# A hybrid decoder layer: the down projection's weight sums on GpSimd's queue, larger operand loads, and a reordered last block

## The chip, the cores and the metric

One core of a Trainium2 chip. The metric is the device time of one execution in microseconds (us); lower is better. Engines: PE (TensorE, matmuls), DVE (VectorE), ACT (ScalarE), POOL (GpSimd) and SP (SyncE), which here only issues DMAs. DMAs are issued in the order of the issuing engine's queue; "SPq" and "POOLq" are those of SP and POOL.

## The reference

One layer on x of 2048 x 1024, float32. Attention and a convolution group share one input projection; their outputs, concatenated, go through one output projection; then comes a SwiGLU network (inner size 2816), which is most of the work.

```python
y = rms_norm(x, g1); u = y @ w_in            # q, k, v and the conv group's input
a = sliding_window_attention(q, k, v, ...)   # window 128, 8 heads on 2
c = conformer_conv(u_conv, ...)              # GLU, depthwise width 31, LN, swish, pointwise
h = x + rms_norm(concat(a, c) @ w_out, g2)
z = rms_norm(h, g3)
f = (silu(z @ w_gate) * (z @ w_up)) @ w_down
out = h + rms_norm(f, g4)
```

## The kernel before, in words

Every float32 product is made of three matmuls of a short format: high times high, high times low, low times high. ACT makes the high part of an operand (line 888), DVE or POOL subtracts it to get the low part (line 892); both together are called a split. The network's products use Strassen's scheme in Winograd's form: seven block products for eight, with sums of blocks as operands. So sums of weight blocks and of activations are needed, and DVE does most of them.

The rows go through the network in two halves. Stages, with the letters that follow @ in names: A projections, B attention, C convolution, J and W the output side, H the split rows for the network, F0 gate/up of the first half (about 650 to 973 us), G0 its down projection (about 964 to 1285), then F2 and G2 for the second half. F keeps its products in DRAM (`mids`, accumulators in `keeps`) and G loads them. Small tasks run in lanes beside a stage, each with a rate at which its instructions are mixed in. One of them, `stage_tsums`, runs in F0: for each of 11 pairs of weight row blocks it loads four blocks of `w_down` (line 1187: two halves of a "wx" tile and two "fc" tiles, 256 KB each), subtracts four times on DVE (line 85) and stores each sum to the DRAM tensor `td` (line 1193), which G0 and G2 read as weights. "wx" has one buffer, "fc" three, so the next pair's loads wait for this pair's stores to land.

A scheduler fixes the order of instructions on each engine ahead of time, by priorities and its own picture of when operands are there. Each engine then runs its list in order, SP too: an SP instruction that waits holds everything behind it. `tied` only gives an instruction a place behind a stage's leading matmul in that order; `after_first(a, b)` orders b behind a.

In `stage_p2` (G), `load(i)` fetches the operand of step i from `mids` (line 1237), before into "at" for the first two steps and "fa" after ("fa" has 4 buffers, which F's stores use too), in G2 into "fc"; weights come in pairs into "mb" or "raw". `split(i)` makes the operand tiles for PE. For the last six steps of G2 the loop order is turned around, so that one block of 128 rows after another is complete; its epilogue takes the sum of squares on ACT (line 1358), multiplies by the gain `gbs[1]`, takes a reciprocal square root of a single column in ten small DVE operations (`rsqrt_one`), and scales and adds the residual twice. `finish` is the epilogue of the other blocks.

Of the kernel before, what the change touches and what calls it, by code (L numbers as in the profile page):

```python
# [13 lines left out]
F32R = mybir.dt.float32r  # L14
BF16 = mybir.dt.bfloat16
I8 = mybir.dt.int8
I32 = mybir.dt.int32
AF = mybir.ActivationFunctionType
ALU = mybir.AluOpType
# [4 lines left out]
D = 1024  # L24
DFF = 2816
P = 128
T = 512
# [5 lines left out]
EPS = 1e-6  # L33
# [4 lines left out]
def layer_kernel(ctx, tc, x, xT, cols, rows, sinks, relb, onehot, w_in, w_four, w_pw, w_out, w_gate, w_up, w_down, out):  # L38
    nc = tc.nc
    ctx.enter_context(nc.allow_non_contiguous_dma(reason="broadcast and skewed constant loads"))  # L40
    cst = ctx.enter_context(tc.tile_pool(name="cst", bufs=1))
# [7 lines left out]
    def nm(s):  # L49
        uid[0] += 1  # L50
        return f"{s}@{lab[0]}_{uid[0]}"
# [3 lines left out]
    def t_(tag, shape, dt=F32):  # L55
        return sb.tile(list(shape), dt, tag=tag, name=nm(tag), bufs=BUFS[tag])
# [4 lines left out]
    def f2(tag, shape=(P, T)):  # L61
        return t_(tag, shape)

    def hl(tag):
        return t_(tag, (P, 2, T), F32R)
# [13 lines left out]
    act = nc.scalar.activation  # L79
# [3 lines left out]
    def dve(op):  # L83
        def emit(*args, **kw):
            r = op(*args, **kw)  # L85
            if not paced[0]:
                pace["main"] = r.ins
            elif pace["main"] is not None and pace["main"] is not pace["tied"]:
                tc.add_manual_dep(
                    r.ins,  # L90
                    pace["main"].name,
                    mybir.DependencyInfo(mybir.DependencyClass.NoSync, mybir.DependencyReason.DATA),
                    reason="conv taps keep pace with the projections",
                )
                pace["tied"] = pace["main"]
            return r

        return emit

    stt = dve(nc.vector.scalar_tensor_tensor)  # L100
    vtt = dve(nc.vector.tensor_tensor)
    vts = dve(nc.vector.tensor_scalar)
    ptt = nc.gpsimd.tensor_tensor
# [9 lines left out]
    def tied(r):  # L113
        if lead_pe[0] is not None and lead_pe[0] is not r:
            after_first(lead_pe[0], r)
        return r
# [49 lines left out]
                stt(y, t, 1.5, y, ALU.add, ALU.mult)  # L166
        return y

    def rsqrt_one(a, b):
        v, y, w, vs = (sm(1) for _ in range(4))  # L170
        stt(v, a, EPS, b, ALU.add, ALU.add)
        vts(y.bitcast(I32), v.bitcast(I32), 1, None, ALU.logical_shift_right)
        vts(y.bitcast(I32), y.bitcast(I32), -1, 0x5F3759DF, ALU.mult, ALU.add)
        vts(vs, v, -(2.0**-13), None, ALU.mult)
        for f, d in ((v, -3.0), (v, -12.0), (vs, 3 * 2.0**-5)):
            stt(w, y, f, y, ALU.mult, ALU.mult)
            stt(y, w, d, y, ALU.add, ALU.mult)
        return y

    def after_first(first, r, how=mybir.DependencyClass.NoSync):  # L180
        tc.add_manual_dep(
            r.ins,
            first.ins.name,
            mybir.DependencyInfo(how, mybir.DependencyReason.DATA),
            reason="order",
        )
# [12 lines left out]
    ident = cst.tile([P, P], F32, name="ident")  # L199
    make_identity(nc, ident)  # L200
    NCOL = cols.shape[1]
    colt = cst.tile([P, NCOL], F32, name="colt")
    nc.sync.dma_start(colt, cols)
    x0, w0 = [], []
    for i in range(4):
        xt = f4("x", (P, 2, T))
# [34 lines left out]
    )  # L241
    kz = cst.tile([P, 2, P + T], F32R, name="kz")
    nc.gpsimd.memset(kz[:, :, 0:P].bitcast(F32), 0.0)
    junk = cst.tile([P, D], BF16, name="junk")
    vtok = cst.tile([P, 5, P], F32, name="vtok")


# [639 lines left out]
    def split_f(x, w):  # L887
        act(w[:, 0], x, AF.Copy)  # L888
        return w
# [290 lines left out]
    def stage_tsums(td):  # L1180
        L = "G0"
        for pr in range(NF // 2):
            lab[0] = L
            wx = f4("wx", (P, 2, T))
            b = [wx[:, 0], wx[:, 1], f2("fc"), f2("fc")]
            for i, (f, n) in enumerate(((0, 0), (0, 1), (1, 0), (1, 1))):
                tied(nc.sync.dma_start(b[i], w_down[2 * pr + f, :, n * T : (n + 1) * T]))
            yield 5
            b11, b12, b21, b22 = b
            for to, o, p_, q_ in ((0, b11, b12, b11), (2, b12, b22, b12), (1, b22, b22, b11), (3, b21, b21, b22)):  # L1190
                lab[0] = L
                vtt(o, p_, q_, ALU.subtract)
                nc.sync.dma_start(td[to, pr], o)
                yield 1

    def finish(L, gb, jobs, pool=True):
        lab[0] = L
        n_ = len(jobs)
        ssq = sm(4)
        for j, (rows_, halves) in enumerate(jobs):  # L1200
            for n in range(2):
                act(junk[:, 0:T], halves[n], AF.Square, scale=D**-0.5, accum_out=ssq[:, 2 * n + j : 2 * n + j + 1])
                vtt(halves[n], halves[n], gb[n], ALU.mult)
            yield 2.0
            lab[0] = L
        vtt(ssq[:, 0:n_], ssq[:, 0:n_], ssq[:, 2 : 2 + n_], ALU.add)
        r = rsqrt(ssq[:, 0:n_], n_, 1, pool and L == "G0")
        for j, (rows_, halves) in enumerate(jobs):
            ht = f4("wx" if L == "G0" else "mid")
            nc.sync.dma_start(ht, h_scr[rows_])  # L1210
            for n in range(2):
                cs = slice(n * T, (n + 1) * T)
                stt(halves[n], halves[n], r[:, j : j + 1], ht[:, cs], ALU.mult, ALU.add)
                nc.sync.dma_start(out[rows_, cs], halves[n])
            yield 2.0
            lab[0] = L

    def stage_p2(ws, am, td, last=False):
        L = f"G{ws[0]}"
        lab[0] = L  # L1220
        npr = NF // 2
        banks = [mm() for _ in range(4)]
        steps = [(ty, pr) for ty in range(7) for pr in range(npr)]
        rawa, rawb, opsd = {}, {}, {}

        def source(ty, pr):
            if ty in (0, 1, 6):
# [4 lines left out]
        def load(i):  # L1232
            if i < len(steps):
                lab[0] = L
                ty, pr = steps[i]
                rawa[i] = f2("fc" if last else "at" if i < 2 else "fa")
                nc.sync.dma_start(rawa[i], am[ty, pr])
                if pr % 2 == 0:
                    rb = t_("raw" if last else "mb", (P, 2, T))
                    for j in range(min(2, npr - pr)):  # L1240
                        nc.sync.dma_start(rb[:, j], source(ty, pr + j))
                        rawb[i + j] = rb[:, j]

        def split(i):
            if i < len(steps):
                lab[0] = L
                b = split_f(rawb[i], hl(("ql" if i >= len(steps) - 4 else "w") if last else "hl"))
                lo(rawb.pop(i), b, False)
                a = split_f(rawa[i], hl("hl"))
                lo(rawa.pop(i), a, False)  # L1250
                opsd[i] = a, b

# [19 lines left out]
        sse = sm(4) if last else None  # L1272
        gbs = []
# [48 lines left out]
                    lf.add(f"E{ws[0]}.{b}", finish(L, gbs, [  # L1322
                        (rows_of(j, 0), (home("c11", "x", j), home("c12", "p", j))) for j in (b - 1, b)], False))

        LAST = 6 if last else 0
        nn = len(steps) - LAST
        for i in range(3):
            load(i)
        split(0)
        split(1)  # L1330
        for i in range(nn):
            ty, pr = steps[i]
            load(i + 3)
            if i + 2 < nn + (LAST > 0):
                split(i + 2)
            for b in range(4):
                lab[0] = L
                chain(i, b, ty == 0 and pr == 0, pr == npr - 1)
                if pr == npr - 1:
                    after(ty, b)  # L1340
                yield 0.69
            del opsd[i]
        if not last:
            return
        for i in range(nn + 3, len(steps)):
            load(i)
        for i in range(nn + 1, len(steps)):
            split(i)
        hts = []
        for b in range(4):  # L1350
            hts.append(f4("chl"))
            nc.sync.dma_start(hts[b], h_scr[rows_of(b, 0)])
        for b in range(4):
            lab[0] = L
            for i in range(nn, len(steps)):
                chain(i, b, False, i == len(steps) - 1)
            ssq = sm(1)
            act(junk[:, 0:T], banks[b], AF.Square, scale=D**-0.5, accum_out=ssq)
            g = f2("fa")
            vtt(g, banks[b], gbs[1], ALU.mult)  # L1360
            yield 0.69 * LAST
            lab[0] = L
            r = rsqrt_one(ssq, sse[:, b : b + 1])
            c = home("c11", "x", b)
            for y, n in ((c, 0), (g, 1)):
                cs = slice(n * T, (n + 1) * T)
                stt(y, y, r, hts[b][:, cs], ALU.mult, ALU.add)
                nc.sync.dma_start(out[rows_of(b, 0), cs], y)

    clk = [0.0]  # L1370
# [69 lines left out]
    PRE_S0, PRE_S2 = 22, 16  # L1440
    H1, H2, H3, H4 = 0, 4, 7, 11
    NH = 24
    JL, JS = 10, 2
    lb = Lane(RB, 0)
    lc = Lane(RC0, LC)
# [75 lines left out]
    td = dr.tile([4, NF // 2, P, T], F32, name="td")  # L1521
    keeps = [dr.tile([PRES[2 * i], P, T], F32, name=f"keeps{i}") for i in range(2)]
    ws, ops = (0, 1), {}
    for n, off in (("B11", 0), ("B21", 4)):
        lh.add(n + ".0", stage_h_plain(ws, ops, n, off), lambda: since(lw, "W0", NH))
    run(stage_w(1, True, 2, "mid", "hl", "at", mm, norm=lambda g: lh.add("N1", g)))
# [85 lines left out]
```

## Time and profile before

| | |
|---|---|
| median of 3 runs | 1929.01 us (1927.28 to 1930.13) |
| profiled execution | 1926.44 us, span 1924.7 us |
| PE busy | 1891.3 us (98%), mean clock granted 0.997 |
| DVE busy | 1492.3 us (78%) |
| ACT busy | 970.1 us (50%) |
| POOL busy | 197.0 us (10%) |
| DMA | 439.35 MB, 228 GB/s on average |

A group or timeline row gives start and length in us, the engine, the line, out<-in by tile names with @stage, and in brackets the engine's idle time before it and what ended that. L85 is the helper that records all of DVE's operations, and L108 all matmuls, so tiles tell them apart. In the rows of a stretch, the busy time of each engine stands with its instruction count in parentheses.

### The profile page before, as it was taken

The numbers are of one execution on the slowest core, as the hardware profiler recorded it, in microseconds if no ns is written. First come the engines' busy times: TensorE is split into PE (matmuls) and PEld (weight loads), VectorE is DVE, ScalarE is ACT, GpSimd is POOL, SyncE is SP. The second block draws the span as 40 slices with busy tenths as digits, with TensorE's granted clock in tenths as the row PEclk, the third lists the DMA queues.
The fourth block names the chain that finished last, engine by engine and source line by source line (L and its number), as shares of the span: only waits on it lengthen the run. The fifth ranks groups of instructions, "written<-read, shape, count | busy, mean of one in ns | idle before, by whom it ended". The sixth has DMA issues, their size and how long they took to land.

```text
span 1924.7 us, 26694 instructions
## 1 busy us (share of the span) xinstructions
PE 1891.3 (98%) x8714; PEld 1531.9 (80%) x8714; DVE 1492.3 (78%) x2796; ACT 970.1 (50%) x1911; POOL 197.0 (10%) x263
## 2 busy tenths in 40 slices
PE   9999999999999999999999999999999999999998
PEld 7777777777778888887877878888888888888886
DVE  6999999887876999988988765787566665455557
ACT  5366445557567433333445573676434333345443
POOL 2010012110000000000000010010033233211000
PEclk9999999999999999999999999999999999999999
DMA  9886757669668775787496696699544543376664
GB/s 332 303 290 229 228 175 225 195 222 340 216 237 282 247 260 188 252 301 239 146 310 217 214 328 219 230 343 324 174 170 151 167 142 121 120 246 193 206 194 156
DMA packets 227707, 439.35 MB, mean 228 GB/s; under 512 B 22728, under 2 KB 48752, under 8 KB 227568
## 3 DMA queue, kind: packets, MB, share of 16 engines
q1 hardware_dynamic: 206256, 403.04, 63.3%
q10 hardware_dynamic: 19392, 28.32, 4.0%
q0 software_dynamic: 1920, 6.29, 0.8%
q8 instruction: 68, 1.11, 0.2%
q14 instruction: 71, 0.58, 0.1%
HBM read 318.54 MB, written 119.02 MB: 227 GB/s over the span
## 4 chain that ended last, share of the span: by engine, by line
PE 75%; DMA 11%; DVE 9%; issue 2%; ACT 1%; SPq 1%; POOL 0%; DVEq 0%; ACTq 0%; POOLq 0%
PE mm@F L108 36%; PE mm@G L108 20%; PE mm@A L108 9%; PE tr@W L108 4%; DVE fc@C L85 2%; PE tr@B L108 2%; PE mm@W L108 2%; PE ct@J L108 1%; DMA hl@A<-x 1%; DVE chl@F L85 1%; DVE w@F L85 1%; DMA mids<-fa@F 1%; DMA td<-fc@G 1%; DMA chl@F<-w_gate 1%; DMA wx@G<-w_down 1%
## 5 line engine op out<-in xcount | busy, mean ns | idle before, releaser
L85 DVE SCALAR_TENSOR_TENSOR fc@C<-glu@C,colt,fc@C 128x512 f32<-128x512 f32 x480 | 352.6, 751 | 1.8
L108 PE MATMUL mm@F<-hl@H,w@F 128*128 128x512 f32 x1056 | 254.4, 390 | 0.7 <-ACT gb@F L1143 0.7
L108 PEld LDWEIGHTS mm@F<-hl@H,w@F 128*128 128x128 f32 x1056 | 198.0, 188 | 42.2 <-ACT gb@F L1143 1.1
L108 PE MATMUL mm@G<-hl@G,hl@G 128*128 128x512 f32 x924 | 225.7, 394 | 4.5 <-ACT hl@G L888 3.8
L888 ACT ACTIVATE w@F<-chl@F 128x512 fp32r<-128x512 f32 x220 | 135.5, 625 | 142.3 <-PE mm@F L108 136.8
L108 PEld LDWEIGHTS mm@G<-hl@G,hl@G 128*128 128x128 f32 x924 | 170.9, 188 | 42.2 <-ACT hl@G L888 4.7
L108 PE MATMUL mm@G<-w@G,hl@G 128*128 128x512 f32 x876 | 199.5, 389 | 0.0
L108 PE MATMUL mm@A<-hl@A,w@A 128*128 128x512 f32 x792 | 191.9, 393 | 1.9 <-DVE w@A L85 1.1
L108 PEld LDWEIGHTS mm@G<-w@G,hl@G 128*128 128x128 f32 x876 | 164.5, 188 | 34.1
L108 PEld LDWEIGHTS mm@A<-hl@A,w@A 128*128 128x128 f32 x792 | 147.0, 188 | 34.9 <-issue 1.7
L85 DVE TENSOR_TENSOR w@F<-chl@F,w@F 128x512 fp32r<-128x512 f32 x198 | 143.8, 730 | 37.0 <-ACT w@F L888 36.6
L108 PE MATMUL mm@F<-ql@H,w@F 128*128 128x512 f32 x528 | 130.3, 391 | 2.9 <-ACT w@F L888 2.9
L108 PE MATMUL mm@F<-mid@H,w@F 128*128 128x512 f32 x528 | 130.3, 389 | 0.5 <-DVE fa@F L85 0.5
L108 PE MATMUL mm@F<-p@H,w@F 128*128 128x512 f32 x528 | 129.0, 389 | 0.0
L108 PE MATMUL mm@F<-x@H,w@F 128*128 128x512 f32 x528 | 128.5, 391 | 0.0
L108 PEld LDWEIGHTS mm@F<-ql@H,w@F 128*128 128x128 f32 x528 | 98.5, 188 | 23.9 <-ACT w@F L888 3.7
L108 PEld LDWEIGHTS mm@F<-x@H,w@F 128*128 128x128 f32 x528 | 98.4, 188 | 22.2 <-ACT w@F L888 0.8
L108 PEld LDWEIGHTS mm@F<-mid@H,w@F 128*128 128x128 f32 x528 | 99.0, 188 | 21.5 <-DVE fa@F L85 0.9
L108 PEld LDWEIGHTS mm@F<-p@H,w@F 128*128 128x128 f32 x528 | 99.0, 188 | 20.7 <-ACT at@F L1146 0.2
L108 PE MATMUL mm@W<-w@W,hl@W 128*128 128x512 f32 x384 | 98.6, 401 | 4.0 <-DVE hl@W L85 1.6
L85 DVE TENSOR_TENSOR w@G<-raw@G,w@G 128x512 fp32r<-128x512 f32 x73 | 50.6, 693 | 66.7 <-ACT w@G L888 65.7
L133 ACT ACTIVATE w@A<-raw@A 128x512 fp32r<-128x512 f32 x104 | 63.2, 624 | 70.7 <-DMA raw@A<-w_in 38.6
(316 smaller groups left out, 3176.9 us busy)
## 6 DMA issues: line engine op xcount, KB each, us to landing
mids<-fa@F SPq DMA_DIRECT2D x154, 256.0 KB, 2.8
raw@A<-w_in SPq DMA_DIRECT2D x52, 512.0 KB, 5.8
w@A<-lo_in SPq DMA_DIRECT2D x84, 256.0 KB, 4.6
fc@G<-mids SPq DMA_DIRECT2D x77, 256.0 KB, 3.4
fa@G<-mids SPq DMA_DIRECT2D x75, 256.0 KB, 4.7
w@W<-lo_out SPq DMA_DIRECT2D x48, 256.0 KB, 4.7
chl@F<-w_gate SPq DMA_DIRECT2D x22, 512.0 KB, 3.8
raw@F<-w_gate SPq DMA_DIRECT2D x22, 512.0 KB, 3.7
```

The costliest lines, as they stand in the source:

```text
L85: r = op(*args, **kw)
L108: r = nc.tensor.matmul(*args, **kw)
L133: act(w[:, 0], raw, AF.Copy)
L888: act(w[:, 0], x, AF.Copy)
```

## The change

Five edits:

1. The loads and stores of `stage_tsums` (44 and 44) are issued by POOL, and the loads lose `tied`.
2. In G0's `load`, the first eight operands come as four 512 KB pairs into "chl" tiles. In G2 the last operands go to "fa" and "mb", and their loads and splits are placed twelve steps earlier (`EARLY`); the last two operand splits use a "yt" tile.
3. In the last block's epilogue, each 128-row block's gain multiply and square root are ordered behind the previous block's last operation (`stored_last`).
4. In `finish`, the gain multiplies of G2 (eight) go to POOL.
5. A small ACT copy of `ident` into `junk` is issued at the very start.

```diff
-    def rsqrt_one(a, b):
+    def rsqrt_one(a, b, behind):
         v, y, w, vs = (sm(1) for _ in range(4))
-        stt(v, a, EPS, b, ALU.add, ALU.add)
+        first = stt(v, a, EPS, b, ALU.add, ALU.add)
+        if behind is not None:
+            after_first(behind, first)
...
+    junk = cst.tile([P, D], BF16, name="junk")
+    act(junk[:, 0:P], ident, AF.Copy)
...
             for i, (f, n) in enumerate(((0, 0), (0, 1), (1, 0), (1, 1))):
-                tied(nc.sync.dma_start(b[i], w_down[2 * pr + f, :, n * T : (n + 1) * T]))
+                nc.gpsimd.dma_start(b[i], w_down[2 * pr + f, :, n * T : (n + 1) * T])
...
                 vtt(o, p_, q_, ALU.subtract)
-                nc.sync.dma_start(td[to, pr], o)
+                nc.gpsimd.dma_start(td[to, pr], o)
...
-                vtt(halves[n], halves[n], gb[n], ALU.mult)
+                (vtt if L == "G0" else ptt)(halves[n], halves[n], gb[n], ALU.mult)
...
-                rawa[i] = f2("fc" if last else "at" if i < 2 else "fa")
-                nc.sync.dma_start(rawa[i], am[ty, pr])
+                if not last and i < 8:
+                    if i % 2 == 0:
+                        pair_ = t_("chl", (P, 2, T))
+                        nc.sync.dma_start(pair_, am[ty, pr : pr + 2].rearrange("j p t -> p j t"))
+                        rawa[i], rawa[i + 1] = pair_[:, 0], pair_[:, 1]
+                else:
+                    rawa[i] = f2("fc" if last and i <= nn else "fa")
+                    nc.sync.dma_start(rawa[i], am[ty, pr])
                 if pr % 2 == 0:
-                    rb = t_("raw" if last else "mb", (P, 2, T))
+                    rb = t_("raw" if last and i <= nn else "mb", (P, 2, T))
...
-                a = split_f(rawa[i], hl("hl"))
+                if last and i == len(steps) - 2:
+                    rest.append(t_("yt", (P, 2, 2, T), F32R))
+                a = split_f(rawa[i], rest[0][:, i % 2] if last and i >= len(steps) - 2 else hl("hl"))
...
-            load(i + 3)
+            if i + 3 < nn + (LAST > 0):
+                load(i + 3)
             if i + 2 < nn + (LAST > 0):
                 split(i + 2)
+            if last and nn - EARLY - 3 <= i < nn - EARLY + LAST - 4:
+                load(i + EARLY + 4)
+            if last and nn - EARLY <= i < nn - EARLY + LAST - 1:
+                split(i + EARLY + 1)
...
-            vtt(g, banks[b], gbs[1], ALU.mult)
+            gained = vtt(g, banks[b], gbs[1], ALU.mult)
+            if b:
+                after_first(stored_last[0], gained)
...
-            r = rsqrt_one(ssq, sse[:, b : b + 1])
+            r = rsqrt_one(ssq, sse[:, b : b + 1], stored_last[0])
...
+                stored_last[0] = stt(y, y, r, hts[b][:, cs], ALU.mult, ALU.add)
```

Line numbers in the new kernel are two to eleven higher here. SP's queue in F0, before (the names: `keeps` are kept accumulators, `raw` and `chl` weights, `gb` an accumulator loaded again):

```order
L1071 DMA chl@F_1435_8497<-w_gate 128x1024
L1193 DMA td<-fc@G_1380_8128 128x512
L1187 DMA wx@G_1412_8337<-w_down 128x512
L1160 DMA mids_4768<-fa@F_1394_8221 128x512
L1193 DMA td<-fc@G_1379_8127 128x512
L1187 DMA wx@G_1412_8337<-w_down 128x512
L1187 DMA fc@G_1413_8338<-w_down 128x512
L1101 DMA gb@F_1427_8434<-keeps_4773 128x512
L1187 DMA fc@G_1414_8339<-w_down 128x512
```

and the new one in F0:

```order
L1074 DMA chl@F_1383_8154<-w_up 128x1024
L1104 DMA gb@F_1375_8081<-keeps_4774 128x512
L1132 DMA fa@F_1367_8037<-mids_4769 128x512
L1072 DMA raw@F_1417_8384<-w_up 128x1024
L1074 DMA chl@F_1400_8264<-w_gate 128x1024
L1163 DMA mids_4769<-fa@F_1359_7990 128x512
L1104 DMA gb@F_1392_8203<-keeps_4774 128x512
```

The loads from `w_down` and the stores to `td` are gone from between F0's own loads and stores. They are now on POOL's queue, one pair of row blocks after another and alone in F0; the first two loads and the first store, which waits for a DVE subtraction, stand ahead of the last two attention masks there.

At the passage from F0 to G0, SP's queue before ends with F0's last stores (`mids<-fa@F`) ahead of the first load into "fa" for G0:

```order
L1166 DMA mids_4768<-fa@F_1539_9231 128x512
L143 DMA raw@W_1692_10068<-w_join 128x2x512
L863 DMA at@W_1745_10378<-x 128x512
L1166 DMA mids_4768<-fa@F_1531_9177 128x512
L1237 DMA fa@G_1560_9419<-mids_4768 128x512
```

and the new one has all four pair loads (`chl@G`, 128x2x512) between F0's stores:

```order
L1244 DMA chl@G_1557_9413<-mids_4769 128x2x512
L1169 DMA mids_4769<-fa@F_1499_8922 128x512
L1163 DMA mids_4769<-fa@F_1503_8962 128x512
L1244 DMA chl@G_1559_9418<-mids_4769 128x2x512
L1169 DMA mids_4769<-fa@F_1501_8942 128x512
L1169 DMA mids_4769<-fa@F_1507_8971 128x512
L1172 DMA mids_4769<-fa@F_1503_8962 128x512
L1244 DMA chl@G_1592_9533<-mids_4769 128x2x512
L143 DMA raw@W_1611_9638<-w_out 128x2x512
L1244 DMA chl@G_1615_9654<-mids_4769 128x2x512
```

The first load into "fa" for G0 stands 30 rows further down, behind F0's last store but one. The last operations of DVE before (`sm` are the small columns of the square root; those numbered 2973 to 2975 belong to the third block, those from 2978 on to the fourth):

```order
L85 TENSOR_TENSOR fa@G_2977_17713<-mm@G_2655_15848,glu@G_2831_16852 128x512
L85 SCALAR_TENSOR_TENSOR sm@G_2978_17715<-sm@G_2976_17711,sm@G_2656_15849 128x1
L85 SCALAR_TENSOR_TENSOR sm@G_2973_17676<-sm@G_2974_17677,sm@G_2973_17676 128x1
L85 TENSOR_SCALAR sm@G_2979_17716<-sm@G_2978_17715 128x1
L85 TENSOR_SCALAR sm@G_2981_17718<-sm@G_2978_17715 128x1
L85 SCALAR_TENSOR_TENSOR sm@G_2974_17677<-sm@G_2973_17676,sm@G_2975_17678 128x1
L85 TENSOR_SCALAR sm@G_2979_17716<-sm@G_2979_17716 128x1
L85 SCALAR_TENSOR_TENSOR sm@G_2973_17676<-sm@G_2974_17677,sm@G_2973_17676 128x1
L85 SCALAR_TENSOR_TENSOR sm@G_2980_17717<-sm@G_2979_17716,sm@G_2978_17715 128x1
L85 SCALAR_TENSOR_TENSOR x@G_2747_16356<-x@G_2747_16356,sm@G_2973_17676,chl@G_2956_17569 128x512
L85 SCALAR_TENSOR_TENSOR fa@G_2971_17673<-fa@G_2971_17673,sm@G_2973_17676,chl@G_2956_17569 128x512
```

and at the same place in the new order:

```order
L85 SCALAR_TENSOR_TENSOR x@G_2743_16349<-x@G_2743_16349,sm@G_2968_17668,chl@G_2951_17561 128x512
L85 SCALAR_TENSOR_TENSOR fa@G_2966_17665<-fa@G_2966_17665,sm@G_2968_17668,chl@G_2951_17561 128x512
L85 TENSOR_TENSOR fa@G_2972_17705<-mm@G_2651_15841,glu@G_2827_16845 128x512
L85 SCALAR_TENSOR_TENSOR sm@G_2973_17707<-sm@G_2971_17703,sm@G_2652_15842 128x1
L85 TENSOR_SCALAR sm@G_2974_17708<-sm@G_2973_17707 128x1
L85 TENSOR_SCALAR sm@G_2976_17710<-sm@G_2973_17707 128x1
```

The third block's two large operations (into `x` and `fa`) now stand ahead of the whole chain of the fourth, where they stood in the middle of it.

More of the change, by code (lines that the diff above doesn't have):

```diff
@@ L243, in layer_kernel @@
     nc.gpsimd.memset(kz[:, :, 0:P].bitcast(F32), 0.0)
-    junk = cst.tile([P, D], BF16, name="junk")
     vtok = cst.tile([P, 5, P], F32, name="vtok")
@@ L1224, in stage_p2 @@
         rawa, rawb, opsd = {}, {}, {}
+        LAST = 6 if last else 0
+        nn = len(steps) - LAST
         def source(ty, pr):
@@ L1323, in after @@
                         (rows_of(j, 0), (home("c11", "x", j), home("c12", "p", j))) for j in (b - 1, b)], False))
-        LAST = 6 if last else 0
-        nn = len(steps) - LAST
+        rest = []
         for i in range(3):
@@ L1344, in stage_p2 @@
             return
[L1345 to L1349, printed above, removed]
+        hts, stored_last = [], [None]
         for b in range(4):
@@ L1366, in stage_p2 @@
                 cs = slice(n * T, (n + 1) * T)
-                stt(y, y, r, hts[b][:, cs], ALU.mult, ALU.add)
+                stored_last[0] = stt(y, y, r, hts[b][:, cs], ALU.mult, ALU.add)
                 nc.sync.dma_start(out[rows_of(b, 0), cs], y)
@@ L1442, in layer_kernel @@
     NH = 24
+    EARLY = 12
     JL, JS = 10, 2
```

## The prediction

> **What bounds the kernel now.** I read the busy table first, then the chain that ended last, the busy time by stretch, and the waits of TensorE (PE) and of SyncE's queue (SPq) in the first gate/up stage.
>
> ```profile
> PE 1891.3 (98%) x8714; PEld 1531.9 (80%) x8714; DVE 1492.3 (78%) x2796; ACT 970.1 (50%) x1911; POOL 197.0 (10%) x263
> ...
> 1322.14 380.83 PE mm@F L108 x1680
> 1710.90 196.53 PE mm@G L108 x867
> ```
>
> PE is busy 98% of the span, and over 380.83 us it runs 1680 matmuls back to back, 226.7 ns each. The change leaves the matmuls as they are. So time is to be had only from PE's stalls and from the two ends; from 1322 on PE's work alone sets the time, until the last matmul. The stretches (columns: stretch, length, busy us and count of PE, weight loads, DVE, ACT, POOL; then clock, DMA share, GB/s) say where PE stalls:
>
> ```profile
> 700.00:780.00 80.00, 80.00 (x355) 66.24 (x354) 77.92 (x127) 32.27 (x57) 0.00 (x0) 1.00 0.64 211
> ...
> 860.00:900.00 40.00, 36.64 (x160) 29.69 (x159) 34.19 (x56) 14.71 (x28) 0.00 (x0) 1.00 0.81 268
> ...
> 980.00:1020.00 40.00, 36.86 (x169) 30.18 (x168) 35.07 (x56) 18.29 (x32) 0.00 (x0) 1.00 0.96 325
> 1885.00:1900.00 15.00, 15.00 (x67) 12.40 (x67) 14.18 (x36) 9.31 (x22) 0.00 (x0) 1.00 0.28 92
> ```
>
> The first gate/up stage loses time near 870 and the first down projection at its start near 990. DVE works 77.92 of 80 us in one stretch: it is the second bound of this stage. POOL does nothing in it. PE's waits in 655 to 970 (us in total, times, longest) sum to 5.1 us:
>
> ```profile
> PE mm@F L108 <- ACT w@F L888: 2.9, 2, 2.3
> PE mm@F L108 <- DVE gb@F L85: 1.0, 1, 1.0
> PE mm@F L108 <- ACT gb@F L1143: 0.7, 1, 0.7
> PE mm@F L108 <- DVE fa@F L85: 0.5, 1, 0.5
> ```
>
> **The weight sums to POOL's queue.** It takes 44 loads and 44 stores out of SP's queue, in which an instruction that waits holds all that stands behind it. In the trace this is the chain around 870, in order of time (start, duration, engine):
>
> ```profile
> 855.56 0.68 DVE L85 TENSOR_TENSOR wx@G<-fc@G,wx@G 128x512 f32<-128x512 f32 x1
> 862.18 0.38 SPq L1193 DMA_DIRECT2D td<-fc@G  x1
> 866.93 0.33 SPq L1187 DMA_DIRECT2D fc@G<-w_down  x1
> 870.70 0.69 DVE L85 TENSOR_TENSOR wx@G<-fc@G,wx@G 128x512 f32<-128x512 f32 x1 [2.41 <-DMA fc@G<-w_down]
> 872.77 1.66 PE L108 MATMUL mm@F<-yt@H,w@F 128*128 128x512 f32 x6 [1.02 <-DVE gb@F L85]
> 876.12 0.47 SPq L1101 DMA_DIRECT2D gb@F<-keeps  x1
> 879.88 0.60 ACT L1132 ACTIVATE mm@F<-gb@F 128x512 f32<-128x512 f32 x1 [9.40 <-DMA gb@F<-keeps]
> 881.08 0.73 PE L108 MATMUL mm@F<-ql@H,w@F 128*128 128x512 f32 x2 [2.34 <-ACT w@F L888]
> ```
>
> The store of a sum (862.18) has to land before its buffer is loaded again (866.93); DVE waits 2.41 us for that load and PE 1.02 behind it. The load of a kept accumulator (876.12) is issued late in the same queue, ACT waits 9.40 us for it, and PE 2.34. So 1.02 + 2.34 = 3.4 of the 5.1 us hang on this queue. Its own waits at these lines are these two and smaller ones:
>
> ```profile
> SPq L1193 <- DVE wx@G L85: 21.5, 16, 3.2
> ...
> SPq L1187 <- DMA td<-fc@G: 16.6, 10, 2.8
> ```
>
> That is 38 us in which SP stood still with other loads behind it. On POOL they hold nobody: it has no other work in this stage. What is queued behind a waiting POOL instruction are further weight sums; the one exception are the last two attention masks, ahead of which two first loads and a store now stand:
>
> ```profile
> 545.66 1.21 DVE L85 TENSOR_TENSOR mid@W<-wx@W,mid@W 128x1024 f32<-128x1024 f32 x1
> ...
> 561.07 2.58 POOL L538 TENSOR_SCALAR_AFFINE_SELECT p@B<-p@B 128x512 f32<-128x512 f32 x2 [17.28 <-ACT p@B L536]
> ```
>
> The loads' buffer is free at 546.87, so they land near 551.5 (4.7 below) and the subtraction that the store waits for follows, well ahead of 561; I count nothing.
>
> What remains is the cycle of one pair of sums: in the trace from DVE's operation at 855.56 to the same one at 870.70, 15.1 us. It holds a store and a load that each wait for a landing. The nearest prices for POOL's queue (columns: size, median us to landing; then busy us and mean ns of an issue):
>
> ```profile
> wx@G<-w_down SPq DMA_DIRECT2D x22, 256.0 KB, 4.7
> fc@G<-w_down SPq DMA_DIRECT2D x22, 256.0 KB, 4.6
> ...
> td<-fc@G SPq DMA_DIRECT2D x22, 256.0 KB, 4.0
> ...
> lo_out<-w@W POOLq DMA_DIRECT2D x16, 256.0 KB, 4.1
> lo_in<-w@A POOLq DMA_DIRECT2D x8, 256.0 KB, 6.3
> ```
>
> ```profile
> L137 POOL DMA_DIRECT2D lo_out<-w@W x16 | 8.9, 554 | 66.1 <-DVE w@W L85 59.1 <-DVE sm@B L85 4.9 <-DVE sm@C L643 2.0
> L349 POOL DMA_DIRECT2D lo_in<-w@A x8 | 6.2, 780 | 14.4 <-DVE w@A L85 14.4
> 300.00:420.00 120.00, 113.76 (x585) 87.05 (x584) 109.89 (x261) 63.75 (x158) 24.31 (x46) 0.99 0.68 214
> ```
>
> I take 4.1 us: these sixteen were issued in 300 to 420, when DVE was busy 109.89 of 120 us and the DMA share was 0.68, as in the stage in question; the eight at 6.3 stood in the start, where all DMAs crowd. At 4.1 the cycle is 15.1 + (4.1 − 4.0) + (4.1 − 4.6) plus two longer issues of about 0.2, so 15 us again; at 6.3 it is 15.1 + 2.3 + 1.7 + 0.9 = 20. DVE's own work between two such pairs, counted in the new order with the trace's durations, is an estimated 13.4 to 15.3 us, so at 4.1 DVE waits little. Of the 3.4 us I count 2.5 as gained and leave 0.9 for a DVE that is still just as near its limit. Bounds: 5.1 gained, or the loss of the first rival.
>
> [...]
>
> **The first down projection's loads.** Before, the third and later operands load into the tiles that the gate/up stage's last stores still hold:
>
> ```profile
> 983.76 2.94 SPq L1237 DMA_DIRECT2D fa@G<-mids  x2
> 989.62 0.63 ACT L888 ACTIVATE hl@G<-fa@G 128x512 fp32r<-128x512 f32 x1 [4.14 <-DMA fa@G<-mids]
> 990.30 2.11 PE L108 MATMUL mm@G<-hl@G,hl@G 128*128 128x512 f32 x8 [3.14 <-ACT hl@G L888]
> ```
>
> Now four pair loads into "chl" stand ahead of those stores, and the first eight steps no longer use "fa". The 3.14 us should mostly go; late next are the weights' splits and the output projection's loads, with a DMA share of 0.96 there. I take 2.5, bounds 3.1 and 0 (the wait moves to another tile).
>
> **The tail.** The last rows before the end, PE's last group and DVE's chain behind it:
>
> ```profile
> 1912.25 2.88 PE L108 MATMUL mm@G<-ql@G,hl@G 128*128 128x512 f32 x12
> ...
> 1916.00 0.68 DVE L85 TENSOR_TENSOR fa@G<-mm@G,glu@G 128x512 f32<-128x512 f32 x1
> ...
> 1918.76 1.05 DVE L85 SCALAR_TENSOR_TENSOR sm@G<-sm@G,sm@G 128x1 f32<-128x1 f32 x5
> ...
> 1920.58 0.74 DVE L85 SCALAR_TENSOR_TENSOR fa@G<-fa@G,sm@G,chl@G 128x512 f32<-128x512 f32 x1
> ```
>
> After PE's end (1912.25 + 2.88 = 1915.13) DVE still finishes the third block between the fourth's small operations, as the order of before shows. In the new order the fourth block's chain is alone: gain multiply at 1916.00, ten small ones at about 0.2 (1.05 for five) and one large one, so the last one starts near 1916.00 + 0.6 + 2.1 + 0.7 = 1919.4, not 1920.58. I take 1.1 us, bounds 1.4 and 0.4 (0.5 if the third block's chain, about 0.6 + 2.1 + 1.4 = 4.1 us of DVE for 17 matmuls or 3.9 us of PE, runs late).
>
> **At no cost.** Eight gain multiplies go from DVE (0.68 each) to POOL, and the last operands load and split twelve steps earlier: both lie in a stretch where PE is busy 15.00 of 15 us, which hides them; if the cover were gone, 8 × 0.68 = 5.4 us of DVE is the most that they move. The early table load:
>
> ```profile
> 4.99 1.28 ACT L320 ACT_TABLE_LOAD   x1 [4.99 <-DMA x@X<-xT]
> 14.89 8.36 DMA x@A<-xT
> ```
>
> 1.28 us go from ACT's first step, but the chain then runs over loads of x, so I count 0, bounds 1.3 gained and 0.
>
> **The sum.** 2.5 + 2.5 + 1.1 = 6.1 us off the profiled execution: span 1924.7 and 1.74 around it, 1926.44, to 1920.3. The median of the runs, 1929.01, is 2.57 above that execution, so 1922.9; I say 1923. All bounds of gain, 5.1 + 3.1 + 1.4 + 1.3 = 10.9, give 1918; with 0.5 + 0 + 0.4 it would be 1928. 0.2% (3.9 us) is about what a measurement of this kernel can tell from no change.
>
> **Rivals.** *POOL's landings become DVE's wait (slower).* At 6.3 us a landing the cycle of 20 us exceeds DVE's 13.4 to 15.3: it waits 5 us in each of some seven pairs, 35 us, of which it has about 15 to spare (34.19 of 40 busy near 870). The 20 left reach PE whole or half: +10 to +20, less 3.6 for the other two terms, 1935 to 1945. It decides from a landing of about 5.1 on, where the cycle passes 17 us (DVE's 15.3 and the 2 in 15 that it has to spare). For it: POOL's 6.3, and DVE near its limit. Against it: the 4.1 beside a busy DVE. Chance 0.24.
>
> *The stalls move (no change).* All four of PE's waits in the stage name ACT or DVE, which have as much to do as before; a new order of splits and loads may open as many gaps as it closes, and the pairs' loads may make the down projection wait for "chl". Then only the tail is left: 1926 to 1931. Chance 0.20.
>
> *The pair loads hold SP (slower).* They stand ahead of the gate/up stage's last stores; if "chl" comes free late, these stores and the output projection's weights wait behind them, at DMA share 0.96: 4 to 8 us on top, 1932 to 1936. Nothing in the trace shows such a wait yet. Chance 0.08.
>
> The forecast has 0.48, with a range of its own of 1918 to 1925. So faster 0.48, same 0.20, slower 0.32. For 8 in 10 the range reaches from 1917 to 1940: it leaves out half of the first rival and little below.
>
> **What would show it.** Right: no wait of SP's queue at the sums' lines; PE's waits in 655 to 970 under 3 us; landings of td on POOL's queue near 4; no wait of 3 us at the first matmuls of G; the last large DVE operation less than 4.5 us behind PE's last matmul (5.45 now). Wrong: DVE waits for w_down or td in the gate/up stage for more than 10 us in all, or new PE stalls between 970 and 1285 as large as those gone.

## The result, and the profile after

The changed kernel is slower: 1938.71 us median (six runs, 1932.14 to 1942.40) against 1927.76 for the kernel before on the same chip (six runs); ratio 1.0048, 95% interval 1.0029 to 1.0067. The forecast was 1923, faster. The profiled execution took 1932.14 us, span 1930.4; it is the fastest of the six: the spans of the two traces differ by 5.7 us, the medians by 11, so about half of the loss is not to be seen in the trace.

The busy table and the chain by engine of the changed kernel (before: PE 75%, DVE 9%):

```profile
PE 1896.6 (98%) x8714; PEld 1534.4 (79%) x8714; DVE 1499.2 (78%) x2788; ACT 970.5 (50%) x1912; POOL 255.0 (13%) x359
...
PE 63%; DVE 19%; DMA 11%; issue 3%; ACT 2%; POOL 1%; SPq 0%; DVEq 0%; ACTq 0%; POOLq 0%
```

PE's idle time, span less busy, is 33.8 us now and was 33.4. What grew is PE's *busy* time, by 5.3 us, for the same matmuls: they ran slower in places. Four stretches, first of before, then of the changed kernel (columns as in the prediction):

```profile
655.00:970.00 315.00, 309.91 (x1362) 254.84 (x1361) 289.60 (x467) 122.64 (x219) 0.00 (x0) 1.00 0.71 235
970.00:1290.00 320.00, 314.34 (x1430) 257.21 (x1429) 243.87 (x429) 191.37 (x342) 21.96 (x72) 1.00 0.79 262
1700.00:1760.00 60.00, 60.00 (x267) 49.69 (x266) 33.95 (x51) 25.61 (x45) 5.48 (x4) 1.00 0.77 258
1900.00:1935.00 35.00, 15.13 (x67) 12.20 (x65) 19.39 (x72) 2.75 (x8) 0.00 (x0) 0.86 0.31 120
```

```profile
655.00:970.00 315.00, 305.28 (x1325) 250.05 (x1324) 281.21 (x453) 121.46 (x217) 36.78 (x68) 0.99 0.67 223
970.00:1290.00 320.00, 316.83 (x1435) 259.11 (x1434) 243.07 (x427) 188.42 (x336) 21.99 (x72) 1.00 0.76 256
1700.00:1760.00 60.00, 57.22 (x246) 46.87 (x245) 37.58 (x55) 28.14 (x48) 5.84 (x4) 0.97 0.86 291
1900.00:1935.00 35.00, 21.92 (x95) 17.30 (x93) 25.36 (x85) 2.75 (x8) 1.03 (x1) 0.91 0.32 121
```

PE got through 37 matmuls fewer in 655 to 970 (8.4 us at 226.7 ns) and 21 fewer in 1700 to 1760 (4.8 us). The first is F0 with the sums on POOL; the second is G2's start, where the prediction had priced nothing. PE's waits in 650 to 968 are now 9.7 us, for 5.1 before:

```profile
PE mm@F L108 <- DVE fa@F L85: 3.4, 1, 3.4
PE mm@F L108 <- DVE gb@F L85: 2.7, 1, 2.7
PE mm@F L108 <- ACT mm@F L1135: 1.5, 2, 1.0
PE mm@F L108 <- ACT fa@F L1156: 1.4, 1, 1.4
PE mm@F L108 <- ACT gb@F L1146: 0.7, 1, 0.7
```

Behind the three longest stalls of these two stretches PE's clock falls. The three rows in the timeline, and then PE alone in stretches of 4 us around them (busy us and count, granted clock, DMA share, GB/s):

```profile
851.15 2.90 PE L108 MATMUL mm@F<-mid@H,w@F 128*128 128x512 f32 x6 [3.38 <-DVE fa@F L85]
...
908.80 1.65 PE L108 MATMUL mm@F<-yt@H,w@F 128*128 128x512 f32 x3 [2.66 <-DVE gb@F L85]
...
1740.05 5.30 PE L108 MATMUL mm@G<-w@G,hl@G 128*128 128x512 f32 x15 [2.78 <-ACT p@G L1281]
```

```profile
852.00:856.00 4.00, 4.00 (x14) 0.74 0.63 234
...
908.00:912.00 4.00, 3.20 (x8) 0.59 0.14 54
...
1740.00:1744.00 4.00, 3.95 (x12) 0.70 0.80 256
```

Six matmuls take 2.90 us where six took 1.66 behind a stall in the trace of before; a full stretch of 4 us holds 17 to 20 matmuls, here 14, 8 and 12. A clock of 0.59 over 4 us is 3.3 us at half speed, (1 − 0.59) / 0.5 x 4, which loses 1.6 us of work. With the stretch beside them (0.84 in 848 to 852, 0.88 in 1744 to 1748) the other two come to 3.4 us each. So each of these stalls cost its own length and about half as much again. In F0, 4.6 us more of waits and two times 1.6 us at half clock make 7.8 of the 8.4 us. Before had one such stretch ahead of its tail, in 360 to 400, where its mean clock is 0.96.

What sets such a fall off is shown by no run. Read in stretches of 0.5 us, the clock inside the three falls is 0.50, for 3.4 us each. Stalls of 2.66 and 2.78 us were followed by one, while one of 3.14 us in the trace of before (990.30) was not: its clock is 1.00 in 988 to 1000.

The landings on POOL's queue in the whole execution (KB, median us):

```profile
wx@G<-w_down POOLq DMA_DIRECT2D x22, 256.0 KB, 4.3
td<-wx@G POOLq DMA_DIRECT2D x22, 256.0 KB, 4.3
fc@G<-w_down POOLq DMA_DIRECT2D x22, 256.0 KB, 4.8
td<-fc@G POOLq DMA_DIRECT2D x22, 256.0 KB, 4.0
```

Over the whole execution they are as fast as SP's were (4.7, 4.0, 4.6, 4.0). Between 790 and 925 us, around F0's stalls, the loads took 4.5 (wx) and 5.2 us (fc) where SP's took 4.4 and 3.8, the stores 4.1 and 4.9 for 4.0 and 4.4. The first rival, landings of 6.3 us, is not what happened. Nor did POOL's issues slow DVE's operations: the 40 sums into fa@F in 655 to 970 took 682 ns each before and 684 after.

### The profile page after: what moved, and what is told of

The parts are those of the page before. It is cut to its first block, busy times and chain, and to the rows that moved or that the text cites. A ratio compares the mean times of both kernels' runs of the same rounds, so it can differ in the third digit from the quotient of the medians.

```text
span 1930.4 us, 26690 instructions
## 1 busy us (share of the span) xinstructions
PE 1896.6 (98%) x8714; PEld 1534.4 (79%) x8714; DVE 1499.2 (78%) x2788; ACT 970.5 (50%) x1912; POOL 255.0 (13%) x359
## 4 chain that ended last, share of the span: by engine, by line
PE 63%; DVE 19%; DMA 11%; issue 3%; ACT 2%; POOL 1%; SPq 0%; DVEq 0%; ACTq 0%; POOLq 0%
PE mm@F L108 35%; PE mm@G L108 16%; DVE fc@C L85 8%; PE tr@W L108 4%; PE mm@A L108 3%; PE mm@W L108 2%; DMA glu@C<-glu_scr 1%; DMA wx@G<-h_scr 1%; DMA mids<-fa@F 1%; DVE sm@G L85 1%; DVE p@B L496 1%; DVE w@F L85 1%; DVE tr@B L493 1%; PE tr@B L108 1%; DMA chl@F<-w_up 1%
## 5 line engine op out<-in xcount | busy, mean ns | idle before, releaser
L133 ACT ACTIVATE w@A<-raw@A 128x512 fp32r<-128x512 f32 x104 | 63.2, 624 | 70.2 <-DMA raw@A<-w_in 33.8
```

The source lines that it names most:

```text
L133: act(w[:, 0], raw, AF.Copy)
```

## The experiments

Each ratio is against the kernel before on the same chip, five rounds, with its 95% interval. The length of F0 is that from F's first matmul to its last, in the one profiled execution of each kernel, so it is a single value: 442.9 us before, 453.3 after.

**POOL's queue or the rest.** First the sums alone on POOL:

```diff
-                tied(nc.sync.dma_start(b[i], w_down[...]))
+                nc.gpsimd.dma_start(b[i], w_down[...])
...
-                nc.sync.dma_start(td[to, pr], o)
+                nc.gpsimd.dma_start(td[to, pr], o)
```

> The kernel before with one edit: the weight sums' 44 loads and 44 stores issued by POOL (and the loads no longer tied). Theory A (the sums on POOL's queue cost the time in F0): slower than before by 5 to 9 us, with PE stalls of 2.5 us and more in 800 to 920 and one or two stretches of 3.4 us at half clock behind them. Theory B (the other edits cost it): within 3 us of before, PE's waits in F0 at most the 5.1 us of before.

Ratio 1.0031 (1.0018 to 1.0044), 1934.12 us; F0 450.1 us. That is theory A, in its signs too: PE stalls of 3.10 us (at 855) and 2.76 us (at 913), and a mean clock of 0.96 in 840 to 880 and in 880 to 920.

The changed kernel with the sums back on SP (the reverse of that diff):

> The changed kernel with the weight sums' loads and stores back on SP's queue; all other edits kept. Theory A: F0 as before, the gain of the down projection's start (3 us) and of the tail (1 to 2 us) against the loss at G2's start (4.5 us), so within 2 us of before. Theory B: slower than before by 5 us and more.

Ratio 0.9982 (0.9971 to 0.9992), 1924.90 us; F0 446.4 us. Without POOL's queue the change is a gain of 3 us, a little more than theory A gave, and theory B's loss did not come. POOL's queue costs 6 us alone (3 to 8 by the interval) and some 13 on top of the other edits (1.0048 against 0.9982; 7 to 19 with both intervals at their ends). Why it costs more there, if it does, is not settled.

**G2's early loads.** The changed kernel without them, and the kernel before with them alone:

```diff
-                    rawa[i] = f2("fc" if last and i <= nn else "fa")
+                    rawa[i] = f2("fc" if last else "fa")
...
-            if last and nn - EARLY - 3 <= i < nn - EARLY + LAST - 4:
-                load(i + EARLY + 4)
-            if last and nn - EARLY <= i < nn - EARLY + LAST - 1:
-                split(i + EARLY + 1)
...
+        for i in range(nn + 3, len(steps)):
+            load(i)
+        for i in range(nn + 1, len(steps)):
+            split(i)
```

> The changed kernel with the last six steps' loads and splits of G2 where they were before. Theory C (their early loads, which the scheduler puts near G2's start, hold up the loads that G2 needs first): faster than the changed kernel by 3 to 5 us, without the 2.78 us stall of PE at 1740 and without the stretch at half clock behind it. Rival: the stall comes from F2's late end, and stays; within 1.5 us of the changed kernel.

> The kernel before with one edit: the last six steps' loads and splits of G2 placed twelve steps earlier in the program. Theory C: slower than before by 3 to 5 us, all of it in the first 40 us of G2 (PE stalls there, perhaps 3.4 us at half clock). Rival: within 1 us of before, PE full through G2.

Without: 1934.59 us, ratio 1.0039 (1.0026 to 1.0053), against 1.0048 with them; PE is 60.00 of 60 us busy in 1700 to 1760. Alone: ratio 1.0024 (1.0012 to 1.0035), 1932.31 us. So the place of theory C is right, and alone its price too (4.4 us by the medians), though the trace of that kernel shows only 2.4 us of it as a stall, at full clock. In the changed kernel the 3 to 5 us did not come back: 1.0039 and 1.0048 lie within each other's intervals. In the profile of the early loads alone, SP's queue among F2's last stores, then PE:

```profile
1718.51 0.32 SPq L1240 DMA_DIRECT2D fa@G<-mids  x1
...
1720.56 0.44 SPq L1240 DMA_DIRECT2D fa@G<-mids  x1
1721.38 0.32 SPq L1240 DMA_DIRECT2D fc@G<-mids  x1
1721.79 0.38 SPq L1240 DMA_DIRECT2D fa@G<-mids  x1
```

```profile
1737.74 7.59 PE L108 MATMUL mm@G<-w@G,hl@G 128*128 128x512 f32 x32 [2.37 <-ACT p@G L1273]
```

The "fa" loads, for steps 72 to 76, are issued between the "fc" loads of the first ten: the scheduler brought them forward to where their buffers became free. Their use begins 71 x 12 matmuls behind G2's first, 193 us, so they stood some 180 us ahead of it, and not the sixteen steps (44 us) of the program's text. The splits of the last operands ("ql", "yt") came forward with them, and ACT takes them in its order, ahead of the copy that PE waits for:

```profile
1724.66 0.63 ACT L888 ACTIVATE ql@G<-mb@G 128x512 fp32r<-128x512 f32 x1 [3.22 <-DMA mb@G<-w_down]
...
1735.14 0.63 ACT L888 ACTIVATE yt@G<-fa@G 128x512 fp32r<-128x512 f32 x1
...
1737.11 0.58 ACT L1273 ACTIVATE p@G<-mm@G 128x512 f32<-128x512 f32 x1
```

So ACT stood 3.22 us for a weight that was needed only at the end, and then waited for loads that were needed at once (0.93 and 1.15 us). In the changed kernel's trace the same wait is 3.26 us, with a DMA share in 1700 to 1760 of 0.86 (0.77 before).

Without the early loads the tail gets longer, though: the last matmuls are not block after block, and with DVE's four chains in sequence the last store is issued late. In the changed kernel without them, PE's last group and SP's last store:

```profile
1912.86 2.88 PE L108 MATMUL mm@G<-ql@G,hl@G 128*128 128x512 f32 x12
...
1924.29 0.33 SPq L1380 DMA_DIRECT2D out<-fa@G  x1
```

From PE's end to the end of the span it is 11.6 us there, 9.6 before, 9.4 with the early loads alone and 7.9 in the changed kernel. So the ordered last block lengthens the tail by 2.0 us without the early operands and shortens it by 1.5 with them, and taking them out gives back less than they cost.

**What is left without both.** Sums on SP, no early loads:

> The changed kernel with two edits undone: the weight sums back on SP's queue, and G2's last loads and splits where they were. What is left: the pair loads, the ordered last block, POOL's gain multiplies, the early table load. If the costs of the two edits undone add up (some 6 us for POOL's queue and 4 to 5 for the early loads, from the first four runs): 6 to 9 us faster than before, near 1920. Rival: the gains only showed where the early loads ordered the last matmuls, so 3 us faster at most.

Ratio 0.9986 (0.9976 to 0.9995), 1926.78 us: the rival. The two costs do not add up; the tail, 11.6 us again, takes 2 us of them back.

**The pair loads alone:**

```diff
-                rawa[i] = f2("fc" if last else "at" if i < 2 else "fa")
-                nc.sync.dma_start(rawa[i], am[ty, pr])
+                if not last and i < 8:
+                    if i % 2 == 0:
+                        pair_ = t_("chl", (P, 2, T))
+                        nc.sync.dma_start(pair_, am[ty, pr : pr + 2].rearrange("j p t -> p j t"))
+                        rawa[i], rawa[i + 1] = pair_[:, 0], pair_[:, 1]
+                else:
+                    rawa[i] = f2("fc" if last else "fa")
+                    nc.sync.dma_start(rawa[i], am[ty, pr])
```

> The kernel before with one edit: G0's first eight operands as four pair loads into chl. If the prediction's second term holds: the 3.14 us stall at G0's start gone and 2 to 4 us faster than before. Rival: the wait moves to another tile, within 1 us of before.

Ratio 0.9970 (0.9958 to 0.9981), 1923.63 us: 5.8 us in the interval's middle, more than expected. In PE's rows at G0's start there is no stall left where 3.14 us stood before:

```profile
984.77 0.39 PE L108 MATMUL tr@W<-w@W,ql@W 128*128 128x512 f32 x1
985.00 3.56 PE L108 MATMUL mm@G<-hl@G,hl@G 128*128 128x512 f32 x15
988.40 1.52 PE L108 MATMUL tr@W<-w@W,ql@W 128*128 128x512 f32 x6
```

**Order or queue.** Taking the loads' tie away lets the scheduler move the first sums ahead, and the queue is another matter. Five kernels: untied on SP; both on POOL, tied; stores alone on POOL; loads alone on POOL, untied and tied.

```diff
-                tied(nc.sync.dma_start(b[i], w_down[...]))
+                nc.sync.dma_start(b[i], w_down[...])            # untied on SP
```

> The kernel before with the loads of the weight sums no longer tied, still on SP's queue. The first three pairs of sums then move ahead in DVE's order as they do with POOL's queue. If POOL's loss came from that new order: slower than before by 4 us and more. If it came from the queue itself: within 2 us of before.

```diff
-                tied(nc.sync.dma_start(b[i], w_down[...]))
+                tied(nc.gpsimd.dma_start(b[i], w_down[...]))    # both on POOL, tied
...
-                nc.sync.dma_start(td[to, pr], o)
+                nc.gpsimd.dma_start(td[to, pr], o)
```

> The kernel before with the weight sums on POOL's queue, but their loads still tied, so that DVE's order of the sums stays close to that of before. If the queue itself costs the time (each pair's loads and stores wait for each other in it): slower than before by 4 to 8 us, DVE waiting 6 us and more for wx. If the new order does: within 2 us of before.

```diff
-                nc.sync.dma_start(td[to, pr], o)
+                nc.gpsimd.dma_start(td[to, pr], o)              # stores alone
```

> The kernel before with only the stores of the weight sums on POOL's queue; the loads stay on SP's, tied. If POOL's loss comes from loads and stores that wait for each other in one queue: within 2 us of before, DVE's waits for DMAs in F0 near 20 us. If it comes from the DMAs of that queue being slower or from any change of order: slower by 3 us and more, DVE's waits 25 us and more.

```diff
-                tied(nc.sync.dma_start(b[i], w_down[...]))
+                nc.gpsimd.dma_start(b[i], w_down[...])          # loads alone, untied
```

> The kernel before with only the loads of the weight sums on POOL's queue, not tied; the stores stay on SP's. If the two kinds holding each other in one queue make the loss: about what the untied loads alone cost (2 to 5 us slower). If the queue's DMAs make it: 5 us and more slower, with DVE's waits for wx and fc above 10 us.

```diff
-                tied(nc.sync.dma_start(b[i], w_down[...]))
+                tied(nc.gpsimd.dma_start(b[i], w_down[...]))    # loads alone, tied
```

> The kernel before with only the loads of the weight sums on POOL's queue, still tied, so that the first pairs of sums stay where they were in DVE's order; the stores stay on SP's queue. If loads on POOL's queue cost time whatever the order: slower than before by 3 us and more, F0 3 us and more longer. If their loss was the moved order of the first pairs: within 2 us of before, F0 between 441 and 446 us.

| loads | stores | ratio to before (95%) | F0, us | DVE's waits for DMAs in F0, us |
|---|---|---|---|---|
| SP, tied (before) | SP | 1 | 442.9 | 20.4 |
| SP, untied | SP | 1.0025 (1.0010 to 1.0040) | 447.6 | 26.4 |
| SP, tied | POOL | 1.0008 (0.9995 to 1.0021) | 446.0 | 22.5 |
| POOL, tied | SP | 1.0019 (1.0006 to 1.0032) | 451.0 | 16.6 |
| POOL, tied | POOL | 1.0020 (1.0007 to 1.0032) | 449.1 | 26.7 |
| POOL, untied | SP | 1.0052 (1.0033 to 1.0071) | 456.0 | 21.2 |
| POOL, untied | POOL | 1.0031 (1.0018 to 1.0044) | 450.1 | 30.4 |

The other kernels with loads tied and both on SP have F0 between 440.9 and 446.4 us. Neither pure theory holds. The stores on POOL cost nothing that can be told; the loads there, tied, cost some 0.2%, with or without the stores; untying them costs 0.25% by itself; both together 0.3 to 0.5%. The theory that a pair's loads and stores hold each other up in one queue falls: the loads alone on POOL are no better than both. Between 790 and 925 us loads there landed in 5.5 (wx) and 5.7 us (fc; medians) with both on POOL, tied, and in 4.7 and 5.3 with the loads alone, untied, against SP's 4.4 and 3.8 before, so that a part of their cost may be the landing. Nor is DVE's waiting the whole of it: in the row "POOL, tied, SP" DVE waits less than before and F0 is 8 us longer; PE waits there 8.5 us, for ACT and DVE. Each of these edits also changes the order that the scheduler makes: the rows of DVE, ACT and PE between 520 and 985 us stand in another order than before in all of them (with the early loads alone, which edit nothing there, they agree), and the stores alone change it least. So queue and order are not parted: a kernel with POOL's queue and the order of before kept was not tried.

**The early loads kept late.** The rest of the change, sums on SP, with G2's early loads tied behind the matmuls of the step before:

```diff
+                    d = nc.sync.dma_start(rawa[i], am[ty, pr])
+                    if last and i > nn:
+                        tied(d)
...
+                        d = nc.sync.dma_start(rb[:, j], source(ty, pr + j))
+                        if last and i > nn:
+                            tied(d)
```

> The changed kernel with the weight sums back on SP's queue, and the early loads of G2's last steps tied behind the matmuls of the step before, so that they stay twelve steps early and no longer go to G2's start. If theory C holds: no PE stall near G2's start, the tail of 8 us kept, and 7 to 10 us faster than before. Rival: the early operands are late by then and PE waits for them near the end; no faster than the pair loads alone (5.8 us).

Ratio 0.9958 (0.9945 to 0.9970), 1921.62 us median, 8.1 us faster than before and the lowest ratio of all; its interval overlaps that of the pair loads alone (0.9958 to 0.9981). The tail is 7.9 us, and PE runs 162 matmuls in a row where the stall was, as theory C has it:

```profile
1706.99 1.52 PE L108 MATMUL mm@F<-mb@H,w@F 128*128 128x512 f32 x6
1708.35 36.88 PE L108 MATMUL mm@G<-w@G,hl@G 128*128 128x512 f32 x162
```

## Why the prediction was wrong

- **The sums on POOL (−2.5 forecast; F0 10 us longer in the trace).** The step that failed is "On POOL they hold nobody", with "at 4.1 DVE waits little" behind it. The price of a landing was right, 4.0 to 4.8 over the whole execution. But the cycle that I closed runs from one subtraction to the same one a pair later, 15 us, and only its length was compared with DVE's work. In the changed kernel it came out at 16.1 to 18.3 us between 818 and 887 (14.4 to 16.7 between 809 and 871 before), with landings of 4.1 to 5.2 us (medians between 790 and 925) for 3.8 to 4.4. And I did not price what else the move does: DVE stands still for other loads as well. Its waits in 650 to 968, of before and then of the changed kernel:

```profile
DVE chl@F L85 <- DMA chl@F<-w_gate: 7.2, 5, 2.2
DVE chl@F L85 <- DMA chl@F<-w_up: 5.8, 6, 1.7
DVE wx@G L85 <- DMA wx@G<-w_down: 0.6, 2, 0.4
```

```profile
DVE chl@F L85 <- DMA chl@F<-w_gate: 12.6, 6, 4.1
DVE chl@F L85 <- DMA chl@F<-w_up: 7.0, 5, 3.9
DVE wx@G L85 <- DMA wx@G<-w_down: 6.7, 3, 3.0
```

  F0's own weight loads come later to DVE, though nothing of the sums stands ahead of them in SP's queue. A queue that waits was not a loss that I could book as a gain: the waits of 38 us were SP's, and SP had no lack of time. Without the sums it waited no less, 256 us in 655 to 970 where it was 216, only at other lines: at those of F0's weight loads (raw, then chl; first before, then after) it stands until DVE has done with the buffers:

```profile
SPq L1069 <- DVE chl@F L85: 16.3, 17, 2.7
SPq L1071 <- DVE w@F L85: 22.6, 18, 3.8
```

```profile
SPq L1072 <- DVE chl@F L85: 55.6, 18, 8.3
SPq L1074 <- DVE w@F L85: 26.4, 17, 5.6
```

  So these loads are issued when DVE frees their buffers, and the move could not bring them forward. Which part of F0's loss comes from POOL's queue and which from the new order of the instructions stays open.
- **PE's stalls in F0.** The chain near 870 did go, 3.4 of the 5.1 us, but the waits in all are 9.7 us; half clock followed two of the new ones, which no step of the prediction held: 2 x 1.6 us.
- **G0's start (−2.5).** Mechanism right, size too small: from F0's end to G0's end 305.1 us after, 310.0 before, and 5.8 us for the pair loads alone. They took nearly all stalls of 970 to 1290, 5.7 us before and 1.0 in the kernel with the pairs alone (3.2 in the changed kernel), not the first one only. And I had read the stall from one execution in which it cost no clock: in the traces of six other kernels with the old loads and the same wait (1.92 to 4.43 us) the eight matmuls behind it took 3.25 to 3.78 us, for 2.11 in that one; in the kernel with untied loads on SP the clock there is 0.50 (992 to 996).
- **The tail (−1.1).** Right: the last large DVE operation starts 4.17 us behind PE's end (5.45 before), the row below; the span's end gains 1.6. What I did not see is that this needs the early operands: without them the serial chain costs 2.0 us.

```profile
1920.96 1.52 PE L108 MATMUL mm@G<-ql@G,yt@G 128*128 128x512 f32 x6
...
1926.65 0.75 DVE L85 SCALAR_TENSOR_TENSOR fa@G<-fa@G,sm@G,chl@G 128x512 f32<-128x512 f32 x1
```

- **"At no cost: both lie in a stretch where PE is busy 15.00 of 15 us".** This step failed outright for the early loads. I took the place from the program's text; the new order of SP's queue had them at G2's start, some 180 us ahead of their use, where they cost 4 to 5 us when alone. For the gain multiplies nothing speaks against it, though they were not run alone: PE is still busy 15.00 of 15 us in 1885 to 1900, with POOL at 8.93.
- **The early table load (0).** Nothing to be seen: F's first matmul came at 525.4 to 532.6 us in five kernels with it, at 527.9 to 531.2 in nine without.
- **The rivals.** "POOL's landings become DVE's wait" had the right sign and edit, and the measured time lies in its 1935 to 1945. Its mechanism is wrong: landings were 4.0 to 4.8 us (4.1 to 5.2 between 790 and 925), not 6.3, and DVE waited 8.8 us for the sums' loads, not 35. "The pair loads hold SP" is refuted.
- **The signs.** Of those named for "right" only one failed, PE's waits in F0 (9.7 us, not under 3). Neither of those named for "wrong" came (8.8 us of DVE's waits for `w_down`, not 10; 3.2 us of stalls in 970 to 1290). They looked at the sums and at G0 alone, so a loss at F0's other loads and at G2's start passed them by.

## What to carry to other kernels

Where a scheduler sets the order, an edit's place is read from the order it makes, for every transfer that the edit issues: a load that is only "earlier" in the text went here as far forward as its buffer allowed, its split with it, and had to be tied to the work that it should follow. A queue that waits a great deal need not cost time: SP's waited 216 us in 655 to 970 in the faster kernel and 256 in the slower. Before moving transfers off it, ask whose late arrival ends a wait on the engine that bounds the stage. And stalls don't simply add up: most of those above 2.5 us, and some of those a little shorter, cost 1.7 us more here, in clock (3.4 us at 0.50).

## What the runs showed of the hardware

DMAs issued by POOL in 655 to 970 us, beside a DVE that was 89% busy (281.21 of 315 us), landed in 3.9 to 4.8 us for 256 KB (medians of the sums' loads and stores); SP's, before, in 4.0 to 4.6. Between 790 and 925 us loads took up to 5.7 us (median) in the kernel with both on POOL, tied. PE stalls of much the same length differed in what came behind them. In 500 to 1300 and 1660 to 1780 us of the fourteen traces, 13 are of 2.2 to 2.5 us: behind five of them PE ran 14 to 16 matmuls in the next 5 us, behind the other eight 21 or 22 (the one at 1737.74 above among these). Of the 18 longer ones all but two (3.03 us, in the changed kernel without early loads, and 3.14 before) had 14 to 16 behind them, or 11, in four cases. In the changed kernel's three the clock was 0.50 for 3.4 us, and so it was behind a stall of 2.78 us in the trace of before (at 381.70). Behind one of 4.43 us at G0's start, with the stores alone on POOL, PE ran 14; one of the four cases is the stall of 4.03 us there in the kernel with untied loads on SP, with 6.8 us at half clock by its rows, (0.08 + 0.50 + 0.27) / 0.5 x 4:

```profile
992.73 3.78 PE L108 MATMUL mm@G<-hl@G,hl@G 128*128 128x512 f32 x8 [4.03 <-ACT hl@G L888]
```

```profile
988.00:992.00 4.00, 0.70 (x4) 0.92 0.90 271
992.00:996.00 4.00, 3.27 (x8) 0.50 1.05 402
996.00:1000.00 4.00, 4.00 (x15) 0.73 1.04 384
```
